# All gate and up panels in rows without the tokens' factor, and the first norm's factors spread by two loads

## The chip, the core and the metric

The kernel runs on one core of a Trainium2 chip. The core has a matrix engine (TensorE, in the profile PE, with its weight loads PEld), a vector engine (VectorE, DVE), a scalar engine (ScalarE, ACT), GpSimd (POOL) and SyncE (SP), which here issues transfers. Matrix products write to the banks of PSUM; everything else works in SBUF. The metric is the device time of one execution in microseconds (us); the median of several runs is compared.

## The reference

One layer of a hybrid decoder for 256 tokens of width 1024, in float32:

```python
h  = rms_norm(x, ln1_g)
q, k, v, z, xbc, dt, gate_a, gate_b = split(h @ w_in)
y_a = moba_attention(norm(q), norm(k), v) @ w_o_attn
y_b = mamba2_mixer(z, xbc, dt, ...) @ w_o_ssm
x  = x + (sigmoid(gate_a) * y_a + sigmoid(gate_b) * y_b) @ w_out
g_ff, u_ff = split(rms_norm(x, ln2_g) @ w_gate_up)     # 2 x 2816 columns
x  = x + (silu(g_ff) * u_ff) @ w_down
x  = x + (p @ w_ple_proj) * sigmoid(rms_norm(x, ln3_g) @ w_ple_gate)
```

`rms_norm(x, g)` is x times g (a factor per column) times the reciprocal root of the mean square of the token's row (a factor per token). Since the factor per token is constant along a row of x, it can be multiplied in before a product with weights or behind it.

## The kernel before, in words

*Products in three parts.* Every float32 operand is split into a rounded high part and a low part (type float32r), and a product is the sum of three: high x high, high x low, low x high. Weights come in chunks of 512 columns and four k-tiles of 128 rows, as two transfers of 512 KB into `raw` (five buffers), issued by SP. ACT rounds each to `wh` (four buffers, L258 to L260), DVE takes the rest to `wl` (six buffers, L260).

*Two forms of a panel.* A panel is a product of all 1024 rows of h with 512 columns of weights. `Panel` (tokens in PSUM's partitions, tiles "g") keeps activations stationary and streams 512 weight columns: two halves of tokens, eight k-tiles, three products each. `Rows` (columns in PSUM's partitions, tiles "gr", four banks) keeps 128 weight columns stationary and streams 512 columns of activations, [high | low] of one k-tile side by side, against the high weights, and the 256 columns of the high part against the low weights. Its sixteen steps (L384 to L398) have four products each, for two k-tiles and one block of 128 columns. Its first half takes the blocks one after the other with all four k-tiles of the half, its second half goes over the blocks twice. After a block's last step ACT evicts it (512 columns) and DVE adds the two halves (L1152).

*Where the tokens' factor goes.* In the token form a token is a partition, and the factor is a scalar operand of the eviction. In the row form tokens lie along the free dimension, so the factor must be a tensor with the 256 factors in every partition.

*The first norm* (`norm_task`, L437). `x_stats` (L414) brings the squares' sums and `rstd1` (two tokens' factors per partition) about when the first two panels end. v, q and k use activations without the factor. For the others the factor is spread over all partitions: ACT multiplies the identity by `rstd1`, the PE multiplies the result by a matrix of ones (`ones_m`), ACT evicts it twice, and DVE multiplies the transposed x by it. Then activations are split anew. The first panel that reads them is a gate panel behind v, q and k.

*The second norm and gate and up.* After the residual (`Residual`, L1046) `split_t` (L990) transposes x, multiplies by the columns' factor and splits it, four k-tiles for each half of the columns. `w_ple_proj`'s two short panels run meanwhile. Then come eleven panels of gate and up, each 256 columns of gate and 256 of up. The first two are a `pair` in token form (L1068): both panels' first halves, then both second halves, so that the second half's activations are needed late. `evac_gu` (L1095) applies `rstd2`, sigmoid and the product; `ff_task` (L1105) transposes the result with four transposes a panel, since `w_down` wants it in rows. While the pair runs, `norm2` (L1120) spreads `rstd2` by another product with ones and multiplies it into new activations (`h2n`), which the nine row panels read. `rows_gu` (L1145) makes silu(gate) x up of each of these from the sums, and splits it.

*What sets the order.* The PE's order is written by a planner (`Filler`, L78). It has a clock, `fill.now`, which each product moves on by its cost, and tasks that wait until the clock has reached their due time; `LAG` (L68) has the waits between a task's parts, in ns of that clock. After each step of a panel at most one due task is emitted. `drain` moves the clock on until a condition holds. A product of a panel follows the one before in the PE's queue (L156), a task's product follows the panel's last one. All other engines' and queues' orders are made by the framework's scheduler, which takes what is ready in its own reckoning by priority: loads and splits of weights ("w") first, then evictions ("ev"), then the tasks ("bg"), then the panels' products. Each queue then runs in the order so fixed and waits where something isn't ready.

Of the kernel before, what the change touches and what calls it, by code (L numbers as in the profile page):

```python
# [16 lines left out]
P = 128  # L17
T = 256
# [47 lines left out]


LAG = {  # L68
    "norm": 0, "norm.x": 7982, "norm.k": 5731, "dt": 3113, "dt.t": 1660, "dt.e": 891, "dt.low": 0,
    "dt.end": 5490, "xbc": 3857, "xbc.t": 2999, "xbc.end": 16627, "z": 0, "z.t": 3129, "z.end": 768,  # L70
    "qk": 15739, "qk.t": 6258, "qk.end": 0, "v": 1782, "cb": 3077, "rows": 0, "prep": 877, "seg": 102,
    "seg.next": 9127, "out": 8638, "out.xdt": 352, "out.end": 545, "off": 3241, "off.end": 51, "finish": 4321,
    "finish.ones": 8093, "sc": 1152, "sc.tr": 1416, "tr": 2000, "tr.val": 0, "val": 5094, "val.end": 1076,
    "m": 811, "res": 3010, "ff": 0, "ff.end": 500, "n2": 1163, "n2.rows": 2102, "n2.k": 0, "gu": 0,
}


# [31 lines left out]
def tile_layer(ctx: ExitStack, tc: tile.TileContext, head, xk, pt, vec, w_dt, w_big, w_dn2, w_pp, out):  # L109
# [13 lines left out]
    sb = ctx.enter_context(tc.tile_pool(name="sb", bufs=1))  # L123
    psg = ctx.enter_context(tc.tile_pool(name="psg", bufs=4, space=bass.MemoryType.PSUM))
    psb = ctx.enter_context(tc.tile_pool(name="psb", bufs=4, space=bass.MemoryType.PSUM))
    fill = Filler()
    uid = [0]

# [67 lines left out]
    with prio("w"):  # L196
# [9 lines left out]
        make_identity(nc, ident)  # L206
        m_tmp = s4([4, P])
        nc.gpsimd.memset(m_tmp[:, 0:3], 1.0)
        ones_m = const.tile([P, P], F32, name="ones_m")
        nc.gpsimd.memset(ones_m, 1.0)  # L210

        nc.gpsimd.affine_select(m_tmp[:, 1], m_tmp[:, 0], pattern=[[-1, P]], compare_op=ALU.is_gt, fill=0.0, base=0, channel_multiplier=1)
        nc.gpsimd.affine_select(m_tmp[:, 2], m_tmp[:, 0], pattern=[[1, P]], compare_op=ALU.is_ge, fill=0.0, base=0, channel_multiplier=-1)
# [165 lines left out]
    class Rows:  # L379
# [6 lines left out]
        def add_all(self, acts, after):  # L386

            for c0 in (0, 4):
                parts = next_chunk()
                runs = [(k0, b) for k0 in (c0, c0 + 2) for b in range(4)]  # L390
                for k0, b in runs if c0 else sorted(runs, key=lambda r: r[1]):
                    cs = slice(b * P, b * P + P)
                    with prio("mm"):
                        for k in (k0, k0 + 1):
                            mm(self.ps[b], parts[k % 4][0][:, cs], acts[k], k == 0, False, main=True)
                        for k in (k0, k0 + 1):
                            mm(self.ps[b][:, :T], parts[k % 4][1][:, cs], acts[k][:, :T], False, k == 7, main=True)
                    fill.now += 52.0  # L398
                    fill.step()
                    if k0 == 6:  # L400
                        after(b, self.ps[b])
# [32 lines left out]
    def xr_of(k):  # L434
        return xraw[k // 2][:, k % 2] if k else x0[:, 8:]

    def norm_task():  # L437
        yield fill.now + LAG["norm"]
        with prio("bg"):
            dg = s2([2, P])  # L440
            for tt in range(2):
                act(dg[:, tt], ident, scale=rstd1[:, tt : tt + 1])
            pr = pb([512])
            mm(pr[:, :T], ones_m, dg.rearrange("p a t -> p (a t)"), True, True)
            rbc = s2([2, T])
            for j in range(2):
                act(rbc[:, j], pr[:, :T])
        for k in range(0, 8, 2):
            with prio("bg"):
                if k:  # L450
                    nc.vector.tensor_mul(xraw[k // 2], xraw[k // 2], rbc)
                else:
                    for j in range(2):
                        nc.vector.tensor_mul(xr_of(j), xr_of(j), rbc[:, 0])
            yield fill.now + LAG["norm.x"]
            with prio("bg"):
                for j in range(k, k + 2):
                    g = g1[:, j : j + 1]
                    act(hn_act[j][0], xr_of(j), scale=g)
                    stt(hn_act[j][1], xr_of(j), g, hn_act[j][0].bitcast(F32), op0=ALU.mult, op1=ALU.subtract)  # L460
            yield fill.now + LAG["norm.k"]
        done.add("norm")
# [6 lines left out]
    e0 = const.tile([P, 32], F32, name="e0")  # L469
    e1t = const.tile([P, P], F32, name="e1t")  # L470
    e1c = const.tile([P, 16, P], F32, name="e1c")
    e1d = ctx.enter_context(tc.tile_pool(name="dram", bufs=1, space=bass.MemoryType.DRAM)).tile([32, P], F32, name="e1d")
    low_h = const.tile([P, P], F32R, name="low_h")
    low_l = const.tile([P, P], F32R, name="low_l")
    done = set()
# [511 lines left out]
        evacuate(kind, i, pan)  # L987


    def split_t(toks, scale_cols, const_scale, acts, delay, tiles=None):  # L990

        th = s4([4, T], F32R)
        tl = s4([4, T], F32R)
        if tiles is not None:
            tiles.append((th, tl))
        yield fill.now + delay
        for jj in range(2):
            with prio("bg"):
# [8 lines left out]
                else:  # L1007
                    for j in range(2):
                        k = 2 * jj + j
                        act(th[:, k], pm[:, j], scale=scale_cols[k])  # L1010
                        stt(tl[:, k], pm[:, j], scale_cols[k], th[:, k].bitcast(F32), op0=ALU.mult, op1=ALU.subtract)
            yield fill.now
        acts.extend((th[:, k], tl[:, k]) for k in range(4))

    for n in range(2):
        with prio("bg"):
# [29 lines left out]
    class Residual:  # L1046


        def __init__(self, base, vcol, dst_rstd):
            self.base, self.vcol, self.dst, self.acts, self.tiles = base, vcol, dst_rstd, [[], []], []  # L1050
            self.ss = const.tile([P, 2, 2], F32, name=nm("ss"))

        def take(self, n, pan):
            b = self.base[n]
            with prio("ev"):
                for tt in range(2):
                    nc.vector.tensor_add(b[:, tt], pan.ps[tt], b[:, tt])
            fill.spawn(split_t([b[:, 0], b[:, 1]], [v[:, self.vcol + 4 * n + k : self.vcol + 4 * n + k + 1] for k in range(4)], None, self.acts[n], LAG["res"], self.tiles), 0)
            with prio("bg"):
                for tt in range(2):  # L1060
                    junk = s2([512])
# [15 lines left out]

    rstd2 = const.tile([P, 2], F32, name="rstd2")
    rstd3 = const.tile([P, 2], F32, name="rstd3")
    res2 = Residual(xin, V_G2, rstd2)  # L1080
    pair(m_act, res2.take)


# [8 lines left out]

    ff = []

    def evac_gu(_, pan):  # L1095
        t = s2([2, T])
        with prio("ev"):
            for tt in range(2):
                r = rstd2[:, tt : tt + 1]
                act(t[:, tt], pan.ps[tt][:, :T], AF.Sigmoid, scale=r)  # L1100
                stt(t[:, tt], pan.ps[tt][:, :T], r, t[:, tt], op0=ALU.mult, op1=ALU.mult)
                stt(t[:, tt], pan.ps[tt][:, T:], r, t[:, tt], op0=ALU.mult, op1=ALU.mult)
        fill.spawn(ff_task(t), 0, LAG["ff"])

    def ff_task(t):  # L1105
        with prio("bg"):
            pm = pb([2, T])
            for tt in range(2):
                for j in range(2):
                    transpose(pm[:, j, tt * P : tt * P + P], t[:, tt, j * P : j * P + P])  # L1110
            f2 = s4([2, 2, T], F32R)
            fh, fl = f2[:, 0], f2[:, 1]
            act(fh, pm)
            nc.vector.tensor_sub(fl, pm, fh.bitcast(F32))
        yield fill.now + LAG["ff.end"]
        ff.extend((fh[:, j], fl[:, j]) for j in range(2))

    h2n = []

    def norm2():  # L1120

        yield fill.now + LAG["n2"]
        with prio("bg"):
            dg = s2([2, P])
            for tt in range(2):
                act(dg[:, tt], ident, scale=rstd2[:, tt : tt + 1])
        yield fill.now + LAG["n2.rows"]
        with prio("bg"):
            pr = pb([512])
            mm(pr[:, :T], ones_m, dg.rearrange("p a t -> p (a t)"), True, True)  # L1130
            rbc = s2([T])
            act(rbc, pr[:, :T])
        for k in range(0, 8, 2):
            yield fill.now + LAG["n2.k"]
            th, tl = (res2.tiles[k // 4][m][:, k % 4 : k % 4 + 2] for m in range(2))
            with prio("bg"):
                t = s2([2, T])
                nc.vector.tensor_add(t, th.bitcast(F32), tl.bitcast(F32))
                nc.vector.tensor_tensor(t, t, rbc.unsqueeze(1).to_broadcast([P, 2, T]), op=ALU.mult)
                h = s4([2, 2, T], F32R)  # L1140
                act(h[:, :, 0], t)
                nc.vector.tensor_sub(h[:, :, 1], t, h[:, :, 0].bitcast(F32))
            h2n.extend(h[:, j].rearrange("p a t -> p (a t)") for j in range(2))

    def rows_gu(i):  # L1145
        gu = s4([4, T])

        def after(b, ps):
            with prio("ev"):
                e = s2([512])  # L1150
                act(e, ps)
                nc.vector.tensor_add(gu[:, b], e[:, :T], e[:, T:])  # L1152
            if b == 3:
                fill.spawn(end(), 0, LAG["gu"])

# [12 lines left out]

        return after

    fill.spawn(norm2(), 0)
    pair(res2.acts, evac_gu)
    h2 = res2.acts[0] + res2.acts[1]
    for i in range(2, 2):
        pan = Panel()
        for hf in range(2):
            pan.add(next_chunk(), h2[4 * hf : 4 * hf + 4], last=hf == 1)
        evac_gu(i, pan)
    fill.drain(lambda: len(h2n) == 8)
    for i in range(2, NFF):  # L1180
        Rows().add_all(h2n, rows_gu(i))

    res3 = Residual(xin, V_G3, rstd3)
    for n in range(2):
# [21 lines left out]
def _layout(i):  # L1206
# [27 lines left out]
    gu = f["w_gate_up"]  # L1234
    gu = np.concatenate([gu[:, :2816].reshape(1024, NFF, 256), gu[:, 2816:].reshape(1024, NFF, 256)], axis=2).reshape(1024, -1)
    big += [chunks(f["w_out"], 512 * n, 4 * g, 4) for g in range(2) for n in range(2)]
    big += [chunks(gu, 512 * n, 4 * g, 4) for g in range(2) for n in range(2)]
    for n in range(2, NFF):
        big += [chunks(gu, 512 * n, 4 * g, 4) for g in range(2)]
    for n in range(2):  # L1240
        big += [chunks(f["w_down"], 512 * n, 4 * c, 4) for c in range(5)]
# [36 lines left out]
```

## Time and profile before

| | |
|---|---|
| median of 3 runs | 584.84 us (584.77 to 585.46) |
| the profiled execution | 585.25 us, its span 583.5 us |
| granted TensorE clock | 1.00 |
| PE, DVE, ACT, POOL busy | 99%, 78%, 64%, 8% of the span |
| memory traffic | 104.97 MB, mean 180 GB/s |

The profile is of one execution. Its span goes from the first to the last instruction; the 1.75 us that the time has beyond it lie around it. Instructions are named by line of the kernel file; helpers have lines of their own: products are L170, transposes L192, all of ACT's activations L151, low parts of weights L260. "SPq" is SP's queue of transfers. A row of the timeline has start, duration, engine, line, operation, tiles written and read, the count of merged instructions, and in brackets the idle time of the engine before it with what ended it.

### The profile page before, as it was taken

Reading aid. Unit: us, or ns where it says so; the run is one execution under the profiler, and the core shown is the slowest. Engines: PE = TensorE matmul, PEld = TensorE weight load, DVE = VectorE, ACT = ScalarE, POOL = GpSimd, SP = SyncE. Lnnn points to the kernel's source line nnn. Section 1 sums busy time; section 2 is a strip of 40 time slices with the busy share of each in tenths; the row PEclk is TensorE's granted clock in tenths of the full one; section 3 lists DMA queues with packets and bytes.
Section 4 is the critical chain, followed back from the end, with each engine's and each line's share of the span. In section 5 each row is a group of like instructions: output and inputs, shape, how many; then the busy total and the mean of one; then the engine's idle time right before and its main releaser. Section 6 shows DMA issues by size and latency. Waiting matters only on the chain.

```text
span 583.5 us, 8612 instructions
## 1 busy us (share of the span) xinstructions
PE 578.3 (99%) x3119; PEld 490.9 (84%) x3119; DVE 457.7 (78%) x745; ACT 373.1 (64%) x582; POOL 47.4 (8%) x44
## 2 busy tenths in 40 slices
PE   9999999999999999999999999999999999999997
PEld 8888888888888888888888888888888888888886
DVE  5686889998998998998898765897777777546464
ACT  7874678676997668666644345766667567535452
POOL 2003100220000311151101000000000000000000
PEclk9999999999999999999999999999999999999999
DMA  8956455476345424435546575555546646565521
GB/s 314 372 188 223 149 182 189 168 194 225 118 154 181 145 79 140 145 111 181 181 144 198 202 258 176 179 181 192 183 163 206 205 153 208 198 202 181 184 71 72
DMA packets 33322, 104.97 MB, mean 180 GB/s; under 512 B 3616, under 2 KB 7040, under 8 KB 33280
## 3 DMA queue, kind: packets, MB, share of 16 engines
q1 hardware_dynamic: 32992, 104.16, 52.9%
q8 instruction: 24, 0.39, 0.3%
q10 hardware_dynamic: 288, 0.26, 0.2%
q14 instruction: 18, 0.15, 0.1%
HBM read 103.28 MB, written 1.06 MB: 179 GB/s over the span
## 4 chain that ended last, share of the span: by engine, by line
PE 99%; DMA 0%; ACT 0%; DVE 0%; issue 0%
PE g L170 52%; PE gr L170 36%; PE pb L170 7%; PE pb L192 3%; DMA x<-in_head 0%; ACT s L151 0%; DVE s L1199 0%; DVE s L1200 0%; ACT wh L151 0%
## 5 line engine op out<-in xcount | busy, mean ns | idle before, releaser
L260 DVE TENSOR_TENSOR wl<-raw,wh 128x1024 fp32r<-128x1024 f32 (+2 forms) x193 | 230.8, 1203 | 90.9 <-ACT wh L151 89.7
L170 PE MATMUL g<-wh,s 128*128 128x512 f32 (+1 forms) x900 | 282.5, 391 | 0.2 <-ACT wh L151 0.2
L151 ACT ACTIVATE wh<-raw 128x1024 fp32r<-128x1024 f32 (+2 forms) x193 | 198.4, 1037 | 131.6 <-PE g L170 81.5
L170 PEld LDWEIGHTS g<-wh,s 128*128 128x128 f32 x900 | 168.8, 189 | 34.7 <-issue 0.5
L170 PE MATMUL gr<-s,wh 128*128 128x512 f32 x608 | 193.5, 399 | 0.0
L170 PE MATMUL g<-wl,s 128*128 128x512 f32 (+1 forms) x450 | 173.3, 387 | 0.0
L170 PEld LDWEIGHTS gr<-s,wl 128*128 128x128 f32 x608 | 114.2, 188 | 26.9
L170 PE MATMUL gr<-s,wl 128*128 128x256 f32 x608 | 119.9, 278 | 0.0
L170 PEld LDWEIGHTS g<-wl,s 128*128 128x128 f32 x450 | 84.4, 188 | 16.4
L170 PEld LDWEIGHTS gr<-s,wh 128*128 128x128 f32 x608 | 93.5, 189 | 1.5 <-issue 0.5
L151 ACT ACTIVATE s<-s 128x512 f32<-128x512 f32 (+2 forms) x49 | 36.6, 747 | 25.4 <-DVE s L1161 15.6
L151 ACT ACTIVATE s<-gr 128x512 f32<-128x512 f32 x76 | 44.3, 592 | 4.2 <-PE gr L170 2.2
L711 POOL TENSOR_SCALAR_AFFINE_SELECT rr<-a_h 128x512 fp32r<-128x512 f32 x16 | 23.8, 1508 | 159.1 <-PE pb L170 118.6
L151 ACT ACTIVATE s<-pb 128x512 f32<-128x512 f32 (+3 forms) x50 | 24.0, 515 | 18.2 <-PE pb L170 12.5
L574 DVE SCALAR_TENSOR_TENSOR s<-s,vecs,s 128x255 f32<-128x255 f32 (+2 forms) x72 | 33.1, 500 | 0.1
L170 PE MATMUL pb<-s,s 128*64 128x128 f32 (+4 forms) x288 | 31.3, 302 | 0.0
L170 PEld LDWEIGHTS pb<-s,s 128*64 128x64 f32 (+1 forms) x288 | 24.7, 154 | 3.9 <-issue 1.2
L192 PE MATMUL pb<-ident,s 128*128 128x128 f32 x170 | 25.0, 273 | 0.0
L406 POOL TENSOR_TENSOR rstd<-tiny,mhalf 128x2 f32<-128x2 f32 x3 | 2.1, 707 | 261.9 <-DVE tiny L405 242.2
L192 PEld LDWEIGHTS pb<-ident,s 128*128 128x128 f32 x170 | 20.3, 141 | 3.0 <-DVE wl L260 0.4
L151 ACT ACTIVATE s<-s,vecs 128x256 f32<-128x256 f32 (+1 forms) x40 | 20.1, 556 | 0.1
L151 ACT ACTIVATE s<-s,tiny,fq 128x128 f32<-128x128 f32 (+1 forms) x32 | 17.1, 537 | 2.0 <-DVE tiny L856 2.0
(146 smaller groups left out, 341.6 us busy)
## 6 DMA issues: line engine op xcount, KB each, us to landing
raw<-in_w_big SPq DMA_DIRECT2D x176, 512.0 KB
raw<-in_head SPq DMA_DIRECT2D x4, 512.0 KB
s<-in_xk SPq DMA_DIRECT2D x4, 512.0 KB
raw<-in_head SPq DMA_DIRECT2D x7, 256.0 KB
e1c<-e1d SPq DMA_DIRECT2D x2, 512.0 KB
raw<-in_w_pp SPq DMA_DIRECT2D x2, 512.0 KB
raw<-in_w_dn SPq DMA_DIRECT2D x2, 512.0 KB
out<-s SPq DMA_DIRECT2D x3, 256.0 KB
```

Of the source, the lines that this page charges most:

```text
L151: return nc.scalar.activation(o, i, f, **kw)
L170: ins = nc.tensor.matmul(o, lhsT, rhs, start=start, stop=stop).ins
L192: queue(nc.tensor.transpose(o, i, ident[: i.shape[0], : i.shape[0]]).ins, False)
L260: nc.vector.tensor_sub(wl, raw, wh.bitcast(F32))
L406: nc.gpsimd.tensor_tensor(dst, t, mhalf[:, : ss.shape[-1]], op=ALU.pow)
L574: stt(cc[:, sft:], u[:, b, : T - sft], cw[3 - sft], cc[:, sft:], op0=ALU.mult, op1=ALU.add)
L711: nc.gpsimd.affine_select(r, bcast(a_h[:, c, h0 : h0 + 4].bitcast(F32), P), pattern=[[0, 4], [1, P]], compare_op=ALU.is_ge, fill=0.0, base ...
```

## The change

The first norm's product with ones goes: `rstd1` is written to a small tensor in DRAM and read back into all partitions, both by ACT's queue. The gate and up panels 0 and 1 are row panels like the other nine. All eleven read the activations that `split_t` makes, without the tokens' factor, laid out as [high | low]; `rstd2` is spread by a write and a read of SP's queue, and DVE multiplies each sum by it. `evac_gu`, `ff_task` and `norm2` are gone, with their product and transposes. The weights of the first two panels are stored in the row panels' order. A row panel whose activations aren't all emitted yet drains the planner ahead of each half. Some lags are changed.

```diff
 LAG = {
-    "norm": 0, "norm.x": 7982, "norm.k": 5731, "dt": 3113, "dt.t": 1660, "dt.e": 891, "dt.low": 0,
+    "spread.w": 3000, "spread.r": 5000, "spread.end": 6000,
+    "norm": 0, "norm.x": 5800, "norm.k": 4600, "dt": 3113, "dt.t": 1660, "dt.e": 891, "dt.low": 0,
...
-    "m": 811, "res": 3010, "ff": 0, "ff.end": 500, "n2": 1163, "n2.rows": 2102, "n2.k": 0, "gu": 0,
+    "m": 811, "res": 3010, "ff.end": 500, "gu": 0,
 }
...
+    rows_d = dram.tile([2, 2, P], F32, name="rows_d")
...
-        ones_m = const.tile([P, P], F32, name="ones_m")
-        nc.gpsimd.memset(ones_m, 1.0)
...
             for c0 in (0, 4):
                 parts = next_chunk()
+                if len(acts) < 8:
+                    fill.drain(lambda: len(acts) >= c0 + 4)
...
+    def spread_write(col, n):
+        (nc.sync if n else nc.scalar).dma_start(rows_d[n].rearrange("t p -> p t"), col)
+
+    def spread_read(dst, n):
+        (nc.sync if n else nc.scalar).dma_start(dst, rows_d[n : n + 1].rearrange("n t p -> n (t p)").unsqueeze(1).to_broadcast([P] + list(dst.shape[1:])))
+
     def norm_task():
         yield fill.now + LAG["norm"]
+        yield fill.now + LAG["spread.w"]
         with prio("bg"):
-            dg = s2([2, P])
-            for tt in range(2):
-                act(dg[:, tt], ident, scale=rstd1[:, tt : tt + 1])
-            pr = pb([512])
-            mm(pr[:, :T], ones_m, dg.rearrange("p a t -> p (a t)"), True, True)
+            spread_write(rstd1, 0)
+        yield fill.now + LAG["spread.r"]
+        with prio("bg"):
             rbc = s2([2, T])
-            for j in range(2):
-                act(rbc[:, j], pr[:, :T])
+            spread_read(rbc, 0)
+        yield fill.now + LAG["spread.end"]
...
-        th = s4([4, T], F32R)
-        tl = s4([4, T], F32R)
+        if rows is None:
+            th = s4([4, T], F32R)
+            tl = s4([4, T], F32R)
+        else:
+            both = [s4([2, 2, T], F32R) for _ in range(2)]
...
-                        act(th[:, k], pm[:, j], scale=scale_cols[k])
-                        stt(tl[:, k], pm[:, j], scale_cols[k], th[:, k].bitcast(F32), op0=ALU.mult, op1=ALU.subtract)
+                        o, ol = (th[:, k], tl[:, k]) if rows is None else (both[jj][:, j, 0], both[jj][:, j, 1])
+                        act(o, pm[:, j], scale=scale_cols[k])
+                        stt(ol, pm[:, j], scale_cols[k], o.bitcast(F32), op0=ALU.mult, op1=ALU.subtract)
...
-    def evac_gu(_, pan):
...
-    def ff_task(t):
...
-    def norm2():
...
                 nc.vector.tensor_add(gu[:, b], e[:, :T], e[:, T:])
+                nc.vector.tensor_mul(gu[:, b], gu[:, b], rbc2[:, 0])
...
-    fill.spawn(norm2(), 0)
-    pair(res2.acts, evac_gu)
...
-    fill.drain(lambda: len(h2n) == 8)
-    for i in range(2, NFF):
-        Rows().add_all(h2n, rows_gu(i))
+    with prio("bg"):
+        rbc2 = s2([1, T])
+        spread_write(rstd2, 1)
+        spread_read(rbc2, 1)
+    for i in range(NFF):
+        Rows().add_all(res2.rows, rows_gu(i))
...
-    big += [chunks(gu, 512 * n, 4 * g, 4) for g in range(2) for n in range(2)]
-    for n in range(2, NFF):
+    for n in range(NFF):
         big += [chunks(gu, 512 * n, 4 * g, 4) for g in range(2)]
```

More of the change, by code (lines that the diff above doesn't have):

```diff
@@ L125, in tile_layer @@
     psb = ctx.enter_context(tc.tile_pool(name="psb", bufs=4, space=bass.MemoryType.PSUM))
+    dram = ctx.enter_context(tc.tile_pool(name="dram", bufs=1, space=bass.MemoryType.DRAM))
+    rows_d = dram.tile([2, 2, P], F32, name="rows_d")
     fill = Filler()
@@ L471, in tile_layer @@
     e1c = const.tile([P, 16, P], F32, name="e1c")
-    e1d = ctx.enter_context(tc.tile_pool(name="dram", bufs=1, space=bass.MemoryType.DRAM)).tile([32, P], F32, name="e1d")
+    e1d = dram.tile([32, P], F32, name="e1d")
     low_h = const.tile([P, P], F32R, name="low_h")
@@ L987, in tile_layer, with split_t @@
         evacuate(kind, i, pan)
-    def split_t(toks, scale_cols, const_scale, acts, delay, tiles=None):
-        th = s4([4, T], F32R)
-        tl = s4([4, T], F32R)
-        if tiles is not None:
-            tiles.append((th, tl))
+    def split_t(toks, scale_cols, const_scale, acts, delay, rows=None):
+        if rows is None:
[3 more added lines that the diff above has]
+            both = [s4([2, 2, T], F32R) for _ in range(2)]
         yield fill.now + delay
@@ L1009, in split_t @@
                         k = 2 * jj + j
-                        act(th[:, k], pm[:, j], scale=scale_cols[k])
-                        stt(tl[:, k], pm[:, j], scale_cols[k], th[:, k].bitcast(F32), op0=ALU.mult, op1=ALU.subtract)
+                        o, ol = (th[:, k], tl[:, k]) if rows is None else (both[jj][:, j, 0], both[jj][:, j, 1])
+                        act(o, pm[:, j], scale=scale_cols[k])
+                        stt(ol, pm[:, j], scale_cols[k], o.bitcast(F32), op0=ALU.mult, op1=ALU.subtract)
             yield fill.now
-        acts.extend((th[:, k], tl[:, k]) for k in range(4))
+        if rows is None:
+            acts.extend((th[:, k], tl[:, k]) for k in range(4))
+        else:
+            rows.extend(both[k // 2][:, k % 2].rearrange("p a t -> p (a t)") for k in range(4))
     for n in range(2):
@@ L1046, in tile_layer, with __init__ @@
     class Residual:
-        def __init__(self, base, vcol, dst_rstd):
-            self.base, self.vcol, self.dst, self.acts, self.tiles = base, vcol, dst_rstd, [[], []], []
+        def __init__(self, base, vcol, dst_rstd, rows=None):
+            self.base, self.vcol, self.dst, self.acts, self.rows = base, vcol, dst_rstd, [[], []], rows
             self.ss = const.tile([P, 2, 2], F32, name=nm("ss"))
@@ L1057, in take @@
                     nc.vector.tensor_add(b[:, tt], pan.ps[tt], b[:, tt])
-            fill.spawn(split_t([b[:, 0], b[:, 1]], [v[:, self.vcol + 4 * n + k : self.vcol + 4 * n + k + 1] for k in range(4)], None, self.acts[n], LAG["res"], self.tiles), 0)
+            fill.spawn(split_t([b[:, 0], b[:, 1]], [v[:, self.vcol + 4 * n + k : self.vcol + 4 * n + k + 1] for k in range(4)], None, self.acts[n], LAG["res"], self.rows), 0)
             with prio("bg"):
@@ L1079, in tile_layer @@
     rstd3 = const.tile([P, 2], F32, name="rstd3")
-    res2 = Residual(xin, V_G2, rstd2)
+    res2 = Residual(xin, V_G2, rstd2, [])
     pair(m_act, res2.take)
@@ L1093, in tile_layer @@
     ff = []
-    def evac_gu(_, pan):
[L1096 to L1103, printed above, removed]
-    def ff_task(t):
[L1106 to L1118, printed above, removed]
-    def norm2():
[L1122 to L1143, printed above, removed]
     def rows_gu(i):
@@ L1169, in rows_gu @@
         return after
-    fill.spawn(norm2(), 0)
-    pair(res2.acts, evac_gu)
[L1173 to L1178, printed above, removed]
-    fill.drain(lambda: len(h2n) == 8)
-    for i in range(2, NFF):
-        Rows().add_all(h2n, rows_gu(i))
+    with prio("bg"):
[4 more added lines that the diff above has]
+        Rows().add_all(res2.rows, rows_gu(i))
     res3 = Residual(xin, V_G3, rstd3)
```

## The prediction, made before the change was run

> **What bounds the kernel.** I read the page's head first, then the waits of the PE, then the chain that ended last in order of time, and last the timelines of VectorE (DVE) and ScalarE (ACT) at the two places that the change touches.
>
> ```profile
> span 583.5 us, 8612 instructions
> ...
> PE 578.3 (99%) x3119; PEld 490.9 (84%) x3119; DVE 457.7 (78%) x745; ACT 373.1 (64%) x582; POOL 47.4 (8%) x44
> ...
> PE 99%; DMA 0%; ACT 0%; DVE 0%; issue 0%
> ```
>
> The first line is the span, the second the busy time by engine, the third the chain by engine. A busy PE alone proves little, since matmul ends are modelled; that the chain, too, is 99% PE is better evidence. The waits of the PE over the whole span (waited for: us in total, times, longest) settle it:
>
> ```profile
> PE pb L200 <- PEq L1267: 0.8, 1, 0.8
> PE g L170 <- ACT wh L151: 0.2, 1, 0.2
> ```
>
> After its start the PE waited once, 0.2 us. So each microsecond of PE work that goes is a microsecond of the end, until something else is late; and work taken from DVE or ACT is worth nothing by itself. The chain in order of time (start, us, what) gives the price of each kind of PE work:
>
> ```profile
> 32.59 0.43 PE pb L170 x2
> ...
> 371.30 5.48 PE g L170 x24
> 376.79 0.43 PE pb L170 x2
> 377.22 17.02 PE g L170 x75
> 394.24 0.22 PE pb L192 x2
> ...
> 399.12 0.22 PE pb L192 x2
> 399.33 96.15 PE gr L170 x552
> 495.49 4.56 PE g L170 x20
> ```
>
> "g" are panels with tokens in PSUM's partitions, "gr" panels in rows, "pb L192" transposes, "pb L170 x2" at 32.59 and 376.79 the two products with ones.
>
> **The change part by part.** *The products with ones.* The rows at 32.59 (first norm) and 376.79 (second) take 0.43 us of the chain each. Both go: 2 x 0.43 = 0.86 us less.
>
> *The transposes.* In the token form each of the two gate and up panels is transposed afterwards by four transposes; they come as four pairs between 394.24 and 399.12, 0.22 us each: 4 x 0.22 = 0.88 us less.
>
> *The two panels in the other form.* A panel has 16 steps either way. A token step is three products of 512 columns, 3 x 17.02/75 = 0.681 us. A row step is two of 512 and two of 256, as many columns, but four instructions: 4 x 96.15/552 = 0.697 us. So 32 steps x 0.016 = 0.51 us more. [...]
>
> *Sum:* -0.86 - 0.88 + 0.51 = -1.23 us on the PE. The profiled execution took 585.25 us around its span of 583.5, 0.41 over the median; it becomes 584.0, and the median 584.84 - 1.23 = 583.6. For bounds: if a row step cost no more than a token step the gain would be 1.74 us; if the cost of the pieces were to hide in neighbours (the PE's 0.2 us of waiting shows there is hardly any slack) and a quarter of both removals were lost, 1.74/4 = 0.44 us, it would be 0.79. I take 1.23, since each of its rows is a stretch of the chain itself.
>
> The rest should cost nothing, each under a named cover.
>
> *The rows' factor for gate and up.* Row panels now take activations without the token factor, and DVE multiplies each 128x256 sum by the factor's rows. Here is one row panel's round on DVE (start, us; idle before it in brackets):
>
> ```profile
> 412.14 2.36 DVE L260 TENSOR_TENSOR wl<-raw,wh 128x1024 fp32r<-128x1024 f32 x2 [0.62 <-ACT wh L151]
> 415.62 1.23 DVE L260 TENSOR_TENSOR wl<-raw,wh 128x1024 fp32r<-128x1024 f32 x1 [1.12 <-ACT wh L151]
> 416.76 1.09 DVE L1152 TENSOR_TENSOR s<-s 128x256 f32<-128x256 f32 x3
> 418.41 1.22 DVE L260 TENSOR_TENSOR wl<-raw,wh 128x1024 fp32r<-128x1024 f32 x1 [0.55 <-ACT wh L151]
> 419.55 0.42 DVE L1152 TENSOR_TENSOR s<-s 128x256 f32<-128x256 f32 x1
> 419.88 0.68 DVE L1160 TENSOR_TENSOR s<-s,s 128x512 f32<-128x512 f32 x1
> 420.60 0.69 DVE L1161 TENSOR_TENSOR s<-s,s 128x512 f32<-128x512 f32 x1
> 421.99 0.69 DVE L1165 TENSOR_TENSOR s<-s,s 128x512 fp32r<-128x512 f32 x1 [0.70 <-ACT s L151]
> 423.29 1.23 DVE L260 TENSOR_TENSOR wl<-raw,wh 128x1024 fp32r<-128x1024 f32 x1 [0.60 <-ACT wh L151]
> ```
>
> A round is 423.29 - 412.14 = 11.15 us, of it 1.12 + 0.55 + 0.70 + 0.60 = 2.97 idle. The multiplication has the shape of the sum at L1152, 0.36 us in a sequence to 0.42 alone: four take 1.45 to 1.68. It fits into the idle time, which shrinks to about 1.3. Behind each on DVE wait the next weights' low parts (L260). They run ahead: the pair that ends at 414.50 serves the panel that starts at 417.4 (seven panels of 11.15 before 495.49 give 417.4), so 2.9 us are in hand.
>
> *The second factor's loads.* They stand on SP's queue: the write waits for the factor, the read for the write, and weight loads wait behind both. The factor is done by
>
> ```profile
> 368.70 0.70 POOL L406 TENSOR_TENSOR rstd<-tiny,mhalf 128x2 f32<-128x2 f32 x1 [52.52 <-DVE tiny L405]
> ```
>
> at 369.40. The first panel starts 96 - 75 = 21 products ahead of 376.79, at 372.0, and its first sum needs the factor after 13 steps, the eviction and the sum, near 372.0 + 9.1 + 1.0 = 382.1. So 12.7 us are there. The nearest rows are the waits of SP for the decays, which go out to memory and return the same way:
>
> ```profile
> SPq L545 <- DMA e1d<-e1t: 4.2, 1, 4.2
> ...
> SPq L715 <- DMA e1c<-e1d: 2.4, 1, 2.4
> ```
>
> 4.2 us for the write and some 2.4 or more for the read: 6.6 to 7 of 12.7. Loads behind them come up to 4.2 us late; there are five raw tiles, a tile is used up per 11.15/4 = 2.8 us, so a load has about 14 us less its landing (2.4 for the same 512 KB) before it is rounded.
>
> *The earlier need of the second norm's activations.* The pair of token panels ran both first halves before it needed a second; a row panel needs all four tiles of a half in its first two steps. DVE delivers them in two groups:
>
> ```profile
> 370.69 1.89 DVE L1011 SCALAR_TENSOR_TENSOR s<-pb,vecs,s 128x256 fp32r<-128x256 f32 x4
> ...
> 374.64 0.87 DVE L1011 SCALAR_TENSOR_TENSOR s<-pb,vecs,s 128x256 fp32r<-128x256 f32 x2
> ```
>
> The first two of the x4 end the first half, at 371.6; the row panel wants them at 372.0 + 0.7 = 372.7 (the pair wanted them at 374.7). The last two, done at 375.5, are wanted at 372.0 + 12 x 0.70 = 380.4. It holds, with 1.1 us in hand at the tightest.
>
> *The first norm's loads.* They replace two small activations and an eviction on ACT by two issues on ACT's queue, and the read must wait there until the write has landed. Queued behind it are the roundings of q's weights:
>
> ```profile
> 24.62 1.06 ACT L151 ACTIVATE wh<-raw 128x1024 fp32r<-128x1024 f32 x1 [1.19 <-DMA raw<-in_w_big]
> 25.59 1.25 ACT L151 ACTIVATE s<-g,rstd 128x512 f32<-128x512 f32 x2
> 26.73 0.69 ACT L151 ACTIVATE s<-ident,rstd 128x128 f32<-128x128 f32 x2
> 27.31 2.00 ACT L151 ACTIVATE wh<-raw 128x1024 fp32r<-128x1024 f32 x2
> 30.12 1.07 ACT L151 ACTIVATE wh<-raw 128x1024 fp32r<-128x1024 f32 x1 [0.81 <-PE g L170]
> ```
>
> ```profile
> 28.39 2.36 DVE L260 TENSOR_TENSOR wl<-raw,wh 128x1024 fp32r<-128x1024 f32 x2 [1.46 <-ACT wh L151]
> ```
>
> The rounding at 30.12 waited for q's first tile to be used up, so its third is wanted twelve products later, at 32.8; its low part, first of the x2 at 28.39, is done at 29.6. In hand: 3.2 us. If the write goes at 25.6, lasts 4.6 (4.2 and its issue) and the read stands ahead of that rounding, the rounding starts at 30.2, 2.9 late: just covered. [...] The planner's lags for this norm add up to 14.0 + 4 x 10.4 = 55.6 us instead of 4 x 13.7 = 54.9, so the gate panel behind it keeps its place in the order of the PE.
>
> **The rivals.** *The first row panel starts too early.* With 1.1 us in hand, one weight rounding (1.07) and its low part (1.23) that slip ahead of the first half's activations make the PE wait 2.3 - 1.1 = 1.2 us: 584.8, no change. For it: rounding has the higher priority and the order is the scheduler's. Against: the order up to 372 stays that of before, less ACT's two multiplications of the identity.
>
> *ACT waits too long for the first write.* A write of W us ends at 25.6 + W; the PE waits for W - 5. At 6 us the result is 584.6, at 7.4 it passes the bound to slower. For it: the scattered write has no row. Against: the scheduler may put roundings between write and read, and only one tile has to slip through.
>
> *DVE becomes the bound of the row panels* (the rival on the other side). DVE's busy time per round becomes 11.15 - 2.97 + 1.68 = 9.86; if of the idle time only the 1.12 shrinks and 0.55 + 0.70 + 0.60 = 1.85 stays, a round takes 11.71, 0.56 over the PE's, and over 11 panels 6.2 us less the 2.9 in hand reach the PE: 583.6 + 3.3 = 586.9. It decides from an idle time of about 1.3 + 2.9/11 = 1.55 us a round. Against: three of the four waits are for a rounding that itself waits for the PE, so a later DVE finds it done; only the 0.70 is rigid.
>
> *The change doesn't shorten the PE's work as said*: excluded, as far as the row and token steps keep their measured pace.
>
> **How the numbers follow.** A difference of 0.2% is 1.17 us, about what a measurement of this kernel can tell from no change, and the forecast lies 0.06 beyond it. The forecast's case has 0.72; its spread (gains of 0.79 to 1.74) falls on both sides, 0.46 faster and 0.26 same. The early row panel has 0.12 (0.10 same, 0.02 slower, if later panels follow), ACT's wait 0.08 (0.05 same, 0.03 slower), DVE as the bound 0.08 (0.01 same, 0.07 slower). Together: faster 0.46, same 0.42, slower 0.12. The forecast's own range is 583.1 to 584.1. With the two milder rivals it reaches to 584.8, and the profiled execution's 0.41 over the median is an uncertainty of either end: 582.7 to 585.2, which leaves out the DVE bound and a long write.
>
> **What would show it.** In the changed profile's chain the x2 pieces of 0.43 us and the four pairs after 394 are gone; w_down's first panel starts 0.43 + 0.37 + 0.43 = 1.2 us earlier, near 494.3; the row stretch has 704 products at 0.174 each; DVE's idle time per round is near 1.3 us and the PE's waits stay under 0.5 us. I'm wrong if the PE waits for "wl", "wh" or the activations near 30, near 372 or in each row panel, or if a row step isn't 0.697 us.

## The result and the profile after

| | before | after |
|---|---|---|
| median of 4 runs | 584.96 us (584.77 to 585.46) | 591.62 us (590.54 to 592.00) |
| ratio, 95% interval | | 1.0105 (1.0090 to 1.0119) |
| the profiled execution | 585.25 us, span 583.5 | 591.66 us, span 589.8 |

The change made the kernel 6.7 us slower, where 1.2 us less was forecast. Single executions scatter, those of the kernel before from 584.77 to 587.25 us in 29; medians are compared.

The head of the page after: span, busy time by engine, granted clock in 40 slices, and the chain that ended last by engine.

```profile
span 589.8 us, 8691 instructions
...
PE 578.7 (98%) x3139; PEld 491.4 (83%) x3139; DVE 465.6 (79%) x781; ACT 370.9 (63%) x577; POOL 48.3 (8%) x43
...
PEclk9997999999999999999999999999999999999999
...
PE 91%; DMA 6%; DVE 1%; SPq 0%; issue 0%; ACT 0%; ACTq 0%; DVEq 0%
```

Two things are new: a dip of the clock in the fourth slice (44 to 59 us), and 6% of transfers in a chain that was all PE before. The PE's waits over the whole span:

```profile
PE g L173 <- ACT wh L154: 4.0, 2, 3.6
PE g L173 <- DVE wl L261: 2.0, 1, 2.0
PE pb L203 <- PEq L1225: 0.8, 1, 0.8
```

Both kinds of wait are for weights, not for activations. The chain in order of time shows what the weights waited for:

```profile
25.67 9.21 DMA rows_d<-rstd
34.88 0.02 issue
34.90 8.72 DMA s<-rows_d
43.62 0.02 issue
43.64 0.43 DVE x L462
...
47.11 1.27 DVE s L468 x3
...
48.44 1.23 DVE wl L261
49.67 0.04 issue
49.71 12.41 PE g L173 x47
...
379.10 122.61 PE gr L173 x704
501.71 3.43 PE g L173 x15
```

The write of the first norm's 256 factors takes 9.21 us, the read 8.72: 17.9 us from `rstd1` to the factor in every partition. Then come DVE's products with it, the new activations' low parts (L468), and only behind these the low part of the weights that the PE wanted. The last two lines are the other half of the change: all eleven gate and up panels in one stretch of 704 products, 122.61/704 = 0.174 each, as forecast. Before, this part ran from 372.0 to 495.49, 123.5 us: here 0.9 was gained. All of the loss was there when it began, at 379.10 instead of 372.0.

ACT's timeline after (idle time in brackets) shows the queue from within; "ACTq" are its issues of transfers:

```profile
25.67 0.39 ACTq L441 DMA_DIRECT2D rows_d<-rstd  x1
...
34.90 0.38 ACTq L444 DMA_DIRECT2D s<-rows_d  x1
35.41 1.06 ACT L154 ACTIVATE wh<-raw 128x1024 fp32r<-128x1024 f32 x1 [4.09 <-PE g L173]
36.38 0.58 ACT L154 ACTIVATE s<-g 128x512 f32<-128x512 f32 x1
44.10 0.51 ACT L154 ACTIVATE s<-x 128x256 fp32r<-128x256 f32 x1 [7.15 <-DVE x L462]
44.52 1.43 ACT L154 ACTIVATE s<-xraw,x 128x256 fp32r<-128x256 f32 x3
45.86 1.99 ACT L154 ACTIVATE wh<-raw 128x1024 fp32r<-128x1024 f32 x2
```

Between 36.96 and 44.10 ACT stands still. Next in its fixed order are four activations of the new h, which need the factor; the rounding of weights of the first k panel that the PE needs (45.86) stands behind them. DVE is held up in the same way:

```profile
43.64 0.43 DVE L462 TENSOR_TENSOR x<-x,s 128x256 f32<-128x256 f32 x1 [5.92 <-DMA s<-rows_d]
...
48.44 2.36 DVE L261 TENSOR_TENSOR wl<-raw,wh 128x1024 fp32r<-128x1024 f32 x2
```

The PE at that place, and four stretches of the span (stretch, its length, busy time of PE, PEld, DVE, ACT and POOL, granted clock, DMA share, GB/s):

```profile
42.92 0.39 PE L173 MATMUL g<-wh,s 128*128 128x512 f32 x1
46.95 0.79 PE L173 MATMUL g<-wh,s 128*128 128x512 f32 x1 [3.65 <-ACT wh L154]
49.71 0.80 PE L173 MATMUL g<-wl,s 128*128 128x512 f32 x1 [1.97 <-DVE wl L261]
```

```profile
27.00:33.00 6.00, 6.00 (x28) 4.95 (x28) 3.77 (x4) 4.10 (x5) 0.00 (x0) 1.00 1.18 64
...
45.00:49.00 4.00, 0.79 (x1) 0.29 (x1) 4.00 (x10) 3.97 (x8) 0.00 (x0) 0.63 0.00 0
49.00:51.00 2.00, 1.29 (x3) 1.10 (x4) 2.00 (x3) 2.00 (x3) 0.00 (x0) 0.50 0.11 23
51.00:53.00 2.00, 2.00 (x6) 1.52 (x6) 2.00 (x4) 0.18 (x1) 0.26 (x1) 0.54 0.83 262
```

The PE lost 3.65 + 1.97 = 5.6 us waiting, and the one product between the waits took 0.79 us instead of 0.23. When it ran again the granted clock was 0.50 to 0.57 until 53, and the 47 products from 49.71 took 12.41 us instead of 47 x 0.227 = 10.7: another 1.7. Together 7.9. At the start of gate and up 7.1 of it are left, since a product with ones of 0.43 is gone and q's first product came 0.4 earlier (26.82, before 27.20). In finer stretches the clock is 1.00 from 42.9 to 45, 0.77 from 45 to 46.9 (the PE stood still since 43.31), 0.50 from 46.9 to 52, 0.57 from 52 to 53 and 1.00 behind it: it came back 3.3 us after the second wait had ended at 49.71.

### The profile page after: what moved, and what is told of

It is laid out like the page before. It is cut to its first block, busy times and chain, and to the rows that moved or that the text cites. A ratio compares the mean times of both kernels' runs of the same rounds, so it can differ in the third digit from the quotient of the medians.

```text
span 589.8 us, 8691 instructions
## 1 busy us (share of the span) xinstructions
PE 578.7 (98%) x3139; PEld 491.4 (83%) x3139; DVE 465.6 (79%) x781; ACT 370.9 (63%) x577; POOL 48.3 (8%) x43
## 4 chain that ended last, share of the span: by engine, by line
PE 91%; DMA 6%; DVE 1%; SPq 0%; issue 0%; ACT 0%; ACTq 0%; DVEq 0%
PE g L173 42%; PE gr L173 40%; PE pb L173 6%; PE pb L195 3%; DMA raw<-in_head 2%; DMA rows_d<-rstd 2%; DMA raw<-in_w_big 2%; DMA s<-rows_d 1%; DVE wl L261 0%; SPq L246 0%; DVE xraw L459 0%; DVE s L468 0%; ACT wh L154 0%; DVE tiny L627 0%; ACT s L154 0%
## 5 line engine op out<-in xcount | busy, mean ns | idle before, releaser
L173 PE MATMUL g<-wh,s 128*128 128x512 f32 (+1 forms) x836 | 263.0, 391 | 4.0 <-ACT wh L154 4.0
L173 PE MATMUL gr<-s,wh 128*128 128x512 f32 x672 | 213.2, 398 | 0.0
L173 PEld LDWEIGHTS g<-wh,s 128*128 128x128 f32 x836 | 157.1, 189 | 36.4 <-ACT wh L154 4.7
L173 PE MATMUL g<-wl,s 128*128 128x512 f32 (+1 forms) x418 | 161.7, 389 | 2.0 <-DVE wl L261 2.0
L173 PEld LDWEIGHTS gr<-s,wl 128*128 128x128 f32 x672 | 126.2, 188 | 29.7
L173 PE MATMUL gr<-s,wl 128*128 128x256 f32 x672 | 132.5, 278 | 0.0
L173 PEld LDWEIGHTS gr<-s,wh 128*128 128x128 f32 x672 | 103.4, 189 | 1.5 <-issue 0.5
L173 PEld LDWEIGHTS g<-wl,s 128*128 128x128 f32 x418 | 78.8, 189 | 17.7 <-DVE wl L261 2.5
L154 ACT ACTIVATE s<-gr 128x512 f32<-128x512 f32 x84 | 49.2, 592 | 5.1 <-PE gr L173 3.8
L154 ACT ACTIVATE s<-pb 128x512 f32<-128x512 f32 (+3 forms) x45 | 21.7, 520 | 11.9 <-PE pb L173 9.2
```

The source lines that it names most:

```text
L154: return nc.scalar.activation(o, i, f, **kw)
L173: ins = nc.tensor.matmul(o, lhsT, rhs, start=start, stop=stop).ins
```

## The experiments

Theory A: the first norm's round trip through DRAM (17.9 us) comes back too late, and the instructions that need it hold up weight splits queued behind them on ACT and DVE. Theory B: the loss comes from the gate and up part. Theory C: the write by pieces crowds the DMA engines, so that weights come late. Where nothing else is said, an edit is made to the kernel after.

**One half of the change each.** e1_gu_only has the gate and up part, and the first norm as before:

```diff
-            spread_write(rstd1, 0)
...
-            spread_read(rbc, 0)
...
+            mm(pr[:, :T], ones_m, dg.rearrange("p a t -> p (a t)"), True, True)
```

> The first norm's factors are spread by the product with ones, as before; gate and up as after the change. Theory A (the loss lies in the first norm's round trip through memory, behind which ACT and DVE hold back the roundings of weights) expects the gate and up part's own worth: the chain from the first gate and up product to the first of w_down took 123.5 us before and 122.6 after, so 584.96 - 0.88 = 584.1 us, and no wait of the PE over 0.5 us. Theory C (the scattered write of four-byte pieces clogs the transfers) expects the same here, since the second norm's write lies in a stretch in which the PE didn't wait. Theory B (the loss is the gate and up part's, with DVE or SP's queue too late) expects 590 us or more.

584.27 us against 585.15, ratio 0.9985 (0.9977 to 0.9994). e2_norm_only is the kernel before with the first norm by loads (the same lines the other way round, with the new lags):

> Gate and up as before; the first norm's factors are spread by ACT's write and read. Theories A and C expect the whole loss and none of the gain: 591.62 + 0.88 = 592.5 us, with the PE waiting 5 to 6 us between 42 and 50 us. Theory B expects 584.96 - 0.43 = 584.5 us.

593.11 us, ratio 1.0135 (1.0122 to 1.0148), with the PE's waits of after, 2.7 us for `wh` and 2.3 for `wl`. The halves add up roughly: -0.9 and +8.0, against 6.7. (Of what e2's profiled execution lost, 1.75 us lie ahead of q's first product, at 28.95 instead of 27.20, and 6.3 behind it.) Theory B falls.

**Another queue.** In e3_sp_queue both of the first norm's transfers stand on SP's queue.

```diff
-        (nc.sync if n else nc.scalar).dma_start(rows_d[n].rearrange("t p -> p t"), col)
+        nc.sync.dma_start(rows_d[n].rearrange("t p -> p t"), col)
```

> The changed kernel with the first norm's write and read on SP's queue in place of ACT's. Theory A expects no help: the round trip is as long, the activations that wait for it stand ahead of the roundings on ACT as in the changed kernel, and SP's read now holds back weight loads too, so 591 us or more. If ACT's queue itself were the cost (the read that blocks ACT until the write has landed), the loss would go: 583.7 to 584.5 us.

591.15 us, 1.0107 (1.0094 to 1.0121), waits of 3.1 and 2.3 us. So the loss doesn't need the read's issue on ACT, which the prediction had watched; the instructions that use what was read do the same harm.

**The dependent instructions later.** e4_late places DVE's products with the factor behind the last low part of weights on DVE, and makes them due later.

```diff
-    "spread.w": 3000, "spread.r": 5000, "spread.end": 6000,
-    "norm": 0, "norm.x": 5800, "norm.k": 4600, "dt": 3113, "dt.t": 1660, "dt.e": 891, "dt.low": 0,
+    "spread.w": 3000, "spread.r": 5000, "spread.end": 24000,
+    "norm": 0, "norm.x": 3400, "norm.k": 2500, "dt": 3113, "dt.t": 1660, "dt.e": 891, "dt.low": 0,
...
-                    nc.vector.tensor_mul(xraw[k // 2], xraw[k // 2], rbc)
+                    follow(nc.vector.tensor_mul(xraw[k // 2], xraw[k // 2], rbc).ins, last_low[0])
```

> The changed kernel with the same write and read on ACT's queue, but the first norm's products with the factor are placed on DVE behind the low part of the weights' tile that was split last, and they are emitted 18 us later on the planner's clock (the lags between the pieces are shorter by as much), so that they and the activations that follow stand behind the roundings of the next panels. Theory A (the order on ACT and DVE is what costs) expects no wait of the PE and the change's full worth on the PE, 584.96 - 0.43 - 0.88 = 583.7 us, although the write still lasts 9 us and the read 8.7. Theory C (the write clogs the transfers, so the weights themselves come late) expects the weights of the second k panel to be late all the same: 3.6 us of waiting or more, 587 us or above.

585.98 us, 1.0023 (1.0012 to 1.0033): 5.6 of the 6.7 us are back, with the transfers as slow as before (write at 25.91, read at 35.10). That is A's mark and not C's (587 or more), but A had expected 583.7 and no wait: 2.3 us are missing against that, 1.7 against e1. The windows show where, at the gate panel, whose last activations are now late: the PE is busy 3.84 of 4 us and 4.51 of 5.

```profile
61.00:65.00 4.00, 3.84 (x20) 2.87 (x18) 4.00 (x8) 4.00 (x10) 0.00 (x0) 1.00 0.63 185
65.00:70.00 5.00, 4.51 (x19) 3.40 (x19) 5.00 (x11) 4.49 (x7) 3.07 (x1) 1.00 0.29 96
```

From the gate panel's first product to the first product of the row panel behind it e4 takes 15.6 us (60.72 to 76.33), e1 13.6 (61.14 to 74.76). Of these 2.0 us, 1.2 lie at the two waits for late activations, where four products start 0.63, 0.34, 0.80 and 0.34 us after the one before instead of 0.227. Another 0.7 lie in the 24 small products ahead of the row panel, which take 2.64 us instead of 1.94.

**A shorter write.** In e5_row_write the PE turns the factors first, so that two rows of 512 bytes are written, not 256 elements of 4.

```diff
-        (nc.sync if n else nc.scalar).dma_start(rows_d[n].rearrange("t p -> p t"), col)
+        pt_r = pb([P])
+        transpose(pt_r[:2], col)
+        row = s2([P])
+        act(row[:2], pt_r[:2])
+        (nc.sync if n else nc.scalar).dma_start(rows_d[n], row[:2])
```

> The changed kernel, but the factors are first turned by one transpose on the PE and evicted by ACT, and each write has two rows of 512 bytes in place of 256 elements of four bytes; reads as in the changed kernel. Theory P (the price of the write goes by its number of pieces) expects the write and its completion to take what the decays' write of 32 rows of 512 bytes took, about 4.6 us from issue to issue, in place of 9.2 and 7.7 us, no crowding of the transfers between 27 and 33 us (over 150 GB/s there, against 64), and with that most of the loss gone: the round trip is 8 to 10 us in place of 18, and the time 584 to 586 us. Theory F (any write to memory and back costs 8 to 9 us, whatever its shape) expects 590 us or more as in the changed kernel.

584.83 us against 585.07, 0.9993 (0.9982 to 1.0003): the loss is gone. It isn't a test of the write alone, since the scheduler made another order with it: a rounding (42.48) and a low part of weights (43.83) now stand between the instructions that use the factor. The timeline of e5, issues of both norms' transfers and ACT's instruction ahead of the first read, then the first use:

```profile
29.98 0.50 ACTq L445 DMA_DIRECT2D rows_d<-s  x1
...
34.55 1.06 ACT L154 ACTIVATE wh<-raw 128x1024 fp32r<-128x1024 f32 x1 [1.66 <-PE g L173]
34.56 0.40 ACTq L448 DMA_DIRECT2D s<-rows_d  x1
...
41.21 0.43 DVE L466 TENSOR_TENSOR x<-x,s 128x256 f32<-128x256 f32 x1 [2.62 <-DMA s<-rows_d]
...
375.84 0.26 SPq L445 DMA_DIRECT2D rows_d<-s  x1
...
377.00 0.33 SPq L448 DMA_DIRECT2D s<-rows_d  x1
```

From the write to the first use it is 11.2 us, not 18.0. From issue to issue it is 4.6 us at the first norm and 1.2 at the second, but the 4.6 aren't the write's: the read stands on ACT behind a rounding that waited for the PE. In the trace the write's last semaphore event comes at 31.09, 1.1 us after its issue, and at the second norm, too, after 1.1 (376.94). The same place of the second norm after, where the write is by elements, and below it that of e6_eight_bytes, whose write goes by 128 pieces of 8 bytes:

```profile
376.52 0.39 SPq L441 DMA_DIRECT2D rows_d<-rstd  x1
...
384.22 0.33 SPq L444 DMA_DIRECT2D s<-rows_d  x1
```

```profile
370.93 0.33 SPq L441 DMA_DIRECT2D rows_d<-rstd  x1
...
374.34 0.33 SPq L444 DMA_DIRECT2D s<-rows_d  x1
```

```diff
-        (nc.sync if n else nc.scalar).dma_start(rows_d[n].rearrange("t p -> p t"), col)
+        (nc.sync if n else nc.scalar).dma_start(rows_d[n].rearrange("t p -> (t p)").rearrange("(p t) -> p t", t=2), col)
```

> The changed kernel, with the two factors of a partition written side by side: 128 pieces of eight bytes in place of 256 of four. The read takes them as they lie, so the factors go to the wrong tokens: that part of the computation is changed, the work is the same. Theory P expects the second norm's write to take clearly less than 7.7 us from issue to issue, near the middle between 4.6 and 7.7, 5 to 6.5 us; theory F expects 7.5 to 8 us.

At the second norm the write of one KB lasts 7.7 us in 256 pieces, 3.4 in 128, 1.2 in two rows; at the first norm 9.2, 5.5 (26.22 to 31.69) and 1.1. The price goes with the pieces, not the bytes, though not in proportion: 5 to 6.5 us had been expected for 128.

e6 is also the plainest test of the first norm's round trip, since its instructions on ACT and DVE, up to 50 us, stand in the order of after. From the write to the first use it is 13.3 us (26.22 to 39.49) instead of 18.0, the PE waits 1.5 us for `wl` instead of 5.6 in all, and its clock is 1.00 from 43 to 50. That is one execution, of 586.05 us.

**Crowding alone.** e9_write_alone is the kernel before with the write by elements added, which nobody waits for.

```diff
         with prio("bg"):
+            nc.scalar.dma_start(rows_d[0].rearrange("t p -> p t"), rstd1)
```

> The kernel before, with one thing added: the first norm's factors are also written out by ACT's queue in 256 pieces of four bytes, and nothing reads them or waits for them. Theory A (the cost is what waits for the round trip) expects no change that can be told, within 0.3 us of the kernel before. Theory C (the write crowds the transfers, and late weights cost by themselves) expects 1 us or more over it.

584.96 us against 584.99, 1.0003 (0.9994 to 1.0012). The window shows the crowd (39 GB/s moved at a DMA share of 0.97), and a PE that doesn't notice it:

```profile
27.00:33.00 6.00, 6.00 (x29) 4.95 (x28) 2.70 (x3) 3.48 (x6) 0.00 (x0) 1.00 0.97 39
```

ACT waits 2.52 us for a raw tile ahead of its rounding at 32.14; weights split before bridge it for the PE. Theory C falls as a cause of its own.

**Late and close together.** e10_late_close is e4 with shorter lags behind the factor ("spread.end" 20000, "norm.x" 1500, "norm.k" 300) and the task's end moved back, so that the gate panel's activations shouldn't be late; e11_row_late is e10 with e5's write of rows; e12_pool_late is e10 with both transfers of the first norm on POOL's queue.

```diff
-        (nc.sync if n else nc.scalar).dma_start(rows_d[n].rearrange("t p -> p t"), col)
+        (nc.sync if n else nc.gpsimd).dma_start(rows_d[n].rearrange("t p -> p t"), col)
```

> As the kernel with the late products, but they start 4 us of the planner's clock earlier and the activations follow each within 1.8 us of it, so that the last ones don't meet the gate panel's need; the task's end is padded so that the gate panel keeps its place. In the late kernel the PE's waits of 5.6 us had gone down to 1.0 us, all of it at 62 to 69 us for the last activations (DVE L469). Theory A expects these to go as well and the whole worth of the change to show: 585.15 - 1.31 = 583.8 us. If the crowded transfers cost something by themselves, 1 us or more of it remains: 584.8 us or more.

> The late and close order of the products with the factor, and the writes in two rows of 512 bytes after a transpose. With the short write the round trip ends near 41 us, and nothing that the PE needs by then stands behind it. Theory A expects the change's worth less two transposes of 0.11 us: 585.1 - 1.31 + 0.22 = 584.0 us, and no wait of the PE over 0.3 us. If a rest of about 1 us stays (584.8 us or more) although the PE doesn't wait in the early stretch, some other part of the first norm's change costs that we haven't named.

> The late and close order, with the first norm's write and read (256 pieces of four bytes, as in the changed kernel) on POOL's queue, behind which nothing is due for 18 us. The write may last as long as on ACT's queue. Theory A expects that ACT, which no longer waits for the write before it issues the read, keeps the roundings in time: 583.8 to 584.2 us. Theory C expects 585 us or more, as in the late and close kernel on ACT's queue (585.3).

| | median, us | ratio, 95% interval |
|---|---|---|
| e10 | 585.34, before 585.07 | 1.0003 (0.9991 to 1.0014) |
| e11 | 584.08, before 584.99 | 0.9983 (0.9975 to 0.9992) |
| e12 | 585.36, before 584.99 | 1.0004 (0.9995 to 1.0013) |

e11 came as expected and is, with e1, the fastest. e10 and e12 missed by over 1 us and came out where theory C had put them; freeing ACT's queue of the read (e12) gave nothing over e10. The chain of e12 shows a cause that isn't C's:

```profile
24.82 9.30 DMA rows_d<-rstd
34.12 0.30 issue
34.42 8.67 DMA s<-rows_d
43.10 0.02 issue
43.12 0.43 DVE x L463
...
56.53 4.21 POOL tiny L643
60.74 0.02 issue
60.76 0.70 DVE s L647
61.47 0.04 issue
61.51 0.88 PE pb L195 x6
```

In e11 these six transposes follow four others at once, one row of ten in the chain:

```profile
59.78 1.09 PE pb L195 x10
```

DVE stood 2.6 us for the read at 43.12. It is behind from there on; it hands the norm of the first k panel to POOL late (56.53, in e11 54.69), POOL works 4.21 us on it (3.07 in e11; why isn't known), and the six transposes start late at 61.51, behind four that ended at 59.94: a wait of 1.6 us of the PE, the same row as in e10 (1.9). None of the lags tried took the 18 us round trip wholly off the PE's path; the shorter write did.

**DVE's room.** e7_dve_twice is e1 with one more product of the same shape on each block's sum, its result unused.

```diff
                 nc.vector.tensor_mul(gu[:, b], gu[:, b], rbc2[:, 0])
+                nc.vector.tensor_mul(e[:, :T], gu[:, b], rbc2[:, 0])
```

> The kernel with gate and up alone changed, and in it one more product of 128x256 on DVE for each block of a row panel (its result isn't used). It measures how far DVE is from being the bound of the row panels. By the prediction's account a round has 11.15 us, 9.86 busy after the change, so another 4 x 0.42 = 1.68 us makes 11.54: 0.39 us over the PE's pace a round, 4.3 us over eleven panels, less 2.9 in hand, 1.4 us or more slower than the kernel with gate and up alone, 585.7 us. If DVE has more in hand than that account says, within 0.3 us of that kernel, 584.3 us.

584.18 us, 0.9981 (0.9970 to 0.9993), the same as e1. In a row panel's round of 11.15 us DVE is busy 8.14 us before, 9.31 after and 10.1 to 10.6 here. DVE isn't the bound of the row panels, with one product or with two.

## Why the prediction was wrong

*The step that failed* is "The first norm's loads", put at no cost under the cover that ACT's roundings had 3.2 us in hand. The text priced the write at 4.6 us, from a write that goes by rows, and found 2.9 of the 3.2 us used: "just covered". Three parts of it were wrong, of which the last decided.

- *The size of the write.* It took 9.2 us, and 9.2 to 12.5 in the variants that kept it on the first norm. The prediction took the row nearest in kind, not in shape: the decays' write of 32 rows of 512 bytes. No row of the kernel before has a write by elements. The runs have: e9 adds one and ACT's queue goes from 288 packets to 560; after it has 832, with pieces of eight bytes (e6) 704, with two rows (e5) 564. The times go the same way: 7.7, 3.4 and 1.2 us from issue to issue for 256, 128 and 2 pieces at the second norm.
- *The read.* The prediction gave it a price for the second norm and none for the first. It took 8.7 us, 6.6 in e5.
- *Who waits.* It looked for the harm behind the read on ACT. In fact 7.15 us of ACT's and 5.92 us of DVE's idle time stand ahead of the instructions that use the factor, and the weights stand behind these. With the transfers on SP's queue it is the same (e3). The read did hold back one rounding on ACT, but without harm: the one at 35.41, whose 4.09 us of idle time the view puts down to the PE, starts at 32.61 in e11, where q's products lie at the same times. Its low part was done at 37.73, and the PE first waited at 43.31, for the next tile. The planner's lags allow 5.0 + 6.0 = 11.0 us from the write to the first use. It was 18.0, and each engine's fixed order passes the difference on to all that stands behind; with 13.3, in the same order (e6), 1.5 us of waiting were left.

*The rival nearest to it*, "ACT waits too long for the first write", with W - 5 us of waiting and a chance of 0.08, has the write right and the mechanism wrong. With W = 9.2 it gives 4.2 us of waiting and 587.8; but q's roundings, which it had wait for the write, ran between write and read (27.45 and 28.96), as its own counterargument had it. That it points the right way is luck: what it lacked is the read, the instructions that use it, and the slow clock behind the wait.

*Held.* The two products with ones, the eight transposes and the row steps: gate and up gained 0.9 us (e1: 585.15 - 584.27), against -0.43 - 0.88 + 0.51 = -0.80. The sum of -1.23 was nearly had where the loads were cured (e11: -0.91, with two transposes of the factors added). The second factor on SP's queue cost nothing, though its write took 7.7 us and not 4.2: the 12.7 us of room held 7.7 and a read. The activations of the second norm came in time; no wait of the PE stands between 372 and 502. The rival with DVE as the bound is refuted (e7); the four products add 1.17 us to DVE's round, not 1.45 to 1.68, and leave 1.84 us idle, not 1.3.

*Open.* e12's profiled execution took 1.58 us more than e11's, its wait of 1.6; by the medians it is 1.3, and e10's median is as far from e11's. Why the small products ahead of e4's first row panel take 0.7 us longer, and POOL 1.1 us longer in e12 than in e11, isn't known. In e5 DVE stands as long for the read as in e12 (2.62 us), but 4.0 us earlier, counted from q's first product (12.4 us behind it against 16.4), and without loss: that it is the hour and not the standing still that counts was not tried by itself. That the slow clock adds 1.7 us to the waits is read off two profiles (in e3 52 products take 13.50 us instead of 11.8); no run took the wait away and kept the clock low.

## What to carry to other kernels

A transfer is to be priced by its pieces before its bytes, as one KB took 7.7, 3.4 and 1.2 us here in 256, 128 and 2 pieces: ask what the contiguous run is on both sides, and turn a column into a row first. In engines with a fixed order, look not at who issues a late transfer but at every instruction that needs its data, and at what is queued behind these on each engine (ACT stood 7.15 us here and DVE 5.92, with weights behind them); a lag in a planner is a promise on a latency, and should be set from a measured one (11.0 us were allowed, 18.0 it took). Two waits of the PE of 3.65 and 1.97 us close together cost 1.7 us more than themselves here, since the clock came back 3.3 us after them.

## What the runs showed of the hardware

- A write of one KB in pieces of 4 bytes lasted 7.0 us (second norm of e12) to 12.5 us (the profiled execution of e10, which took 587.13 us), in two rows of 512 bytes 1.1 us at either norm (e5, e11). The write in pieces held the DMA engines: from 27 to 33 us after has a DMA share of 1.18 with 64 GB/s moved. The same stretch has 0.63 and 207 GB/s in the kernel before, and with rows of 512 bytes (e5) 0.49 and 163 GB/s:

```profile
27.00:33.00 6.00, 6.00 (x28) 5.01 (x27) 3.59 (x3) 3.38 (x5) 0.00 (x0) 1.00 0.63 207
...
27.00:33.00 6.00, 6.00 (x29) 4.84 (x28) 2.53 (x3) 4.36 (x6) 0.00 (x0) 1.00 0.49 163
```

- The queue that issues it shows no difference: 9.2 to 12.5 us from ACT, 9.3 from POOL (e12), 11.2 to the read's issue from SP (e3, 24.28 to 35.43).
- The load of 256 KB behind it landed after 6.0 us (e10) to 9.0 (e4), after 8.7 in the kernel after; behind the write of rows after 6.6 (e5) and 7.4 (e11). The runs don't tell the two apart.
- The granted clock fell to 0.50 (after, 46.9 to 52 us; the PE's waits there are 3.65 us, to 46.95, and 1.97 us, to 49.71), and to 0.55 (e3, 48 to 51) behind waits of 2.65 and 2.26; beside one wait of 1.5 to 1.9 (e6, e12, e10) it was 1.00. Over the whole span it was 0.993 in the profiled execution after and 0.996 in that of e3, against 0.999 to 1.00 in those of e6, e10 and e12.
- A part of the scatter of single executions lies at the start. In e2 the first four products of 512 columns take 1.91 us (7.43), the next four 1.08 (9.89); in e5 they take 1.91 (7.38) and 1.09 (9.69); in e11 the first four take 1.09 (6.39). q's first product comes at 28.95 in e2 and 28.79 in e5, at 26.7 to 27.6 in all other profiles.
